# Two decoder layers on one core: 1/rms of the pre-norms moved behind the projections

## The chip, the core and the metric

The kernel runs on one core of one Trainium2 chip. The metric is the time of one execution in device microseconds (us); the median of several runs counts. The core's engines work in parallel, each through its own list of instructions in order: TensorE (PE: matmuls and transposes into PSUM; PEld is its loading of weights), VectorE (DVE), ScalarE (ACT), GpSimd (POOL) and SyncE (SP), which here only issues the DMA transfers. An instruction waits on semaphores for what it reads and for the buffer that it writes.

## The reference, cut to what matters

Two layers; x is 256 positions by 1024 columns, all in float32. Five norms stand in a layer. The three pre-norms (ahead of the mixer, the FFN and the gate) are the subject of the change; the two post-norms are touched on the side.

```python
def rms_norm(x, g, eps=1e-6):
    return x * rsqrt(mean(x * x, axis=-1) + eps) * g

for i in range(2):
    h = rms_norm(x, pre_mix_norm[i])                       # pre-norm 1
    z = h @ w_in[i]                                        # 1024 -> 2560 columns
    z_a, z_b, z_c, z_d = split(z, [768, 1280, 1792])
    out_a = rms_norm(moba_attention(rope(qa), rope(ka), va), out_norm_a[i])
    out_b = rms_norm(spatial_gating(gelu(z_b), ...), out_norm_b[i])
    out_c = rms_norm(conformer_conv(z_c, ...), out_norm_c[i])    # GLU, depthwise conv of 31 taps, ...
    out_d = diff_attention(rope(qd), rope(kd), vd)               # two softmax maps, per-head norm
    y = concat(out_a, out_b, out_c, out_d) @ w_out[i]
    x = x + rms_norm(y, post_mix_norm[i])                  # post-norm 1
    u = causal_dwconv(rms_norm(x, pre_ffn_norm[i]) @ w_up[i], ...)   # pre-norm 2; 5632 columns, 3 taps
    g, val = split(u, 2)
    f = (gelu(g) * val) @ w_down[i]
    x = x + rms_norm(f, post_ffn_norm[i])                  # post-norm 2
    gate = sigmoid(rms_norm(x, pe_gate_norm[i]) @ w_pe_gate[i])      # pre-norm 3
    x = x + gate * (p[i] @ w_pe_proj[i])
```

## The kernel before, in words

**Precision and weights.** A float32 matmul is made of three in the rounded type fp32r: each operand is split into hi (its rounding) and lo (the rest), and `mm3` (L322) adds hi·hi, hi·lo and lo·hi in PSUM. All weights are streamed once, in 208 pieces of 128x1024 (512 KB). For a piece `prep` (L297) issues the load (raw), ScalarE writes hi, and lo = raw - hi is formed by VectorE or, for the 71 pieces listed in POOL (L32), by GpSimd.

**Stages.** The positions lie as two row tiles t = 0, 1 of 128; x stays in SBUF (xs). A layer runs through `mixer` (L459; its steps in the order of the string STEPS, L36), `ffn` (L848) and `gate` (L907). The mixer's projections are made by `tok` (rows = positions: va and vd, bu and bv) or by `feat` (rows = features: the conv input ca and cg; dq, dk, aq, ak, which go through `rope`, L644). In the trace the y matmuls are the output projection, pj the small projection p[i] @ w_pe_proj, u the FFN's first projection (`up(j)`: 48 matmuls of 128x256 into one PSUM tile of 512 columns, for each of 22 j), f the second, gt the gate.

**A norm before.** For a row tile, ScalarE sums squares of two halves (`sumsq`, L413); GpSimd makes 1/rms (`rstd_of`, L403: mean plus eps, then a power of -0.5; in the trace a `_v` and a `_r`); VectorE multiplies xs by 1/rms and by the weight row g in two instructions of 128x512 (`norm_half`, L423: the tiles n_h, nf_h, ng_h for the three pre-norms); TensorE transposes the result in eight blocks of 128x128 into two PSUM tiles (n_t, nf_t, ng_t); ScalarE then writes hi and VectorE lo from PSUM, one 128x512 instruction each for every PSUM tile (`split_out`, L419: h_hi and h_lo, hf_, g_). The matmuls of the next stage read these, a block of 128 rows at a time. The weight rows g are loaded for each norm, 512 KB each (`load_gain`, L341).

**A post-norm before.** `post_norm_half` (L443) sums the squares of the two PSUM tiles of a row tile, multiplies them by g into SBUF tiles (pm_u for the mixer, pf_u for the FFN), and adds the product with 1/rms (pm_r, pf_r) to xs.

**The FFN's chain per j.** When the 48 u matmuls are done, ScalarE writes two uc of 128x256 from the PSUM tile (first tap and bias), VectorE adds four taps from PSUM (uc, 255 or 254 columns); then the PSUM tile is free. Gelu (ScalarE), product (VectorE), hi (ScalarE) and lo (VectorE) of f follow.

**Buffers.** PSUM has four tiles for y, f and gt, two for u and the mixer's projections (tag z) and two for transposes and small products (tag c). u j and u j+2 share a tile.

**Order.** The operations are recorded as the code runs (class Prog, L128), then issued in an order written out by hand, the string ORDER at the end of the file: a list of tokens such as `v.xs`, for the engine (s: ScalarE and the DMA issues of SyncE, v: VectorE, g: GpSimd, t: TensorE) and the tile. Every instruction therefore carries line L230, where `issue` ends up, and is told apart by its tiles. What each engine does in which order is decided by this string alone.

## Time and profile before

| | |
|---|---|
| median of 3 runs | 692.46 us (692.08 to 692.58) |
| profiled execution | 694.2 us |
| its span, first to last instruction | 692.5 us |
| mean granted TensorE clock | 0.992 |
| matmuls (transposes among them) | 4324 |
| HBM read | 118.23 MB, 172 GB/s over the span with the 1.05 MB written |
| weight pieces: load, hi, lo on VectorE, lo on GpSimd | 208, 208, 137, 71 |

In the profile's rows a group of instructions is given as engine, operation, output tile, "<-", input tiles and shape. In a list of groups the number, the busy us in all and the mean ns of one follow, then the idle time of the engine just before them with what ended it. In a stretch of the timeline a row begins with the start in us and the length, and ends with the count; a bracket holds how long the engine had waited and for whom. A table by stages has the window, its length, then for each engine the busy us and the number of instructions, the granted clock, the DMA share and GB/s. Layer 0 has its mixer from 0 to about 137 us, its FFN to about 320 and its gate to about 345; layer 1 follows in the same order.

### The profile page before, as it was taken

The numbers are of one execution on the slowest core, as the hardware profiler recorded it, in microseconds if no ns is written. First come the engines' busy times: TensorE is split into PE (matmuls) and PEld (weight loads), VectorE is DVE, ScalarE is ACT, GpSimd is POOL, SyncE is SP. The second block draws the span as 40 slices with busy tenths as digits, with TensorE's granted clock in tenths as the row PEclk, the third lists the DMA queues.
The fourth block names the chain that finished last, engine by engine and source line by source line (L and its number), as shares of the span: only waits on it lengthen the run. The fifth ranks groups of instructions, "written<-read, shape, count | busy, mean of one in ns | idle before, by whom it ended". The sixth has DMA issues, their size and how long they took to land.

```text
span 692.5 us, 11469 instructions
## 1 busy us (share of the span) xinstructions
PE 655.5 (95%) x4324; PEld 590.1 (85%) x4324; DVE 504.3 (73%) x873; ACT 414.6 (60%) x753; POOL 240.0 (35%) x181
## 2 busy tenths in 40 slices
...
GB/s 326 367 218 147 152 124 92 209 160 140 188 223 173 200 190 186 229 94 189 217 210 186 204 160 122 92 182 123 116 219 206 181 191 149 222 208 168 79 28 62
DMA packets 33750, 120.02 MB, mean 173 GB/s; under 512 B 3872, under 2 KB 4256, under 8 KB 33696
## 3 DMA queue, kind: packets, MB, share of 16 engines
...
HBM read 118.23 MB, written 1.05 MB: 172 GB/s over the span
## 4 chain that ended last, share of the span: by engine, by line
PE 42%; DVE 10%; ACT 2%; issue 1%; POOL 1%; POOLq 0%; DVEq 0%
PE u L230 16%; PE f L230 10%; PE gt L230 7%; DVE lo L230 2%; PE y L230 2%; DVE cacc L230 2%; DVE uc L230 1%; PE ca L230 1%; PE v L230 1%; PE cg L230 1%; PE aq L230 1%; PE ak L230 1%; DVE f L230 1%; DVE sw L230 1%; DVE nf_h L230 1%
## 5 line engine op out<-in xcount | busy, mean ns | idle before, releaser
L230 POOL TENSOR_TENSOR lo<-raw,hi 128x1024 fp32r<-128x1024 f32 x71 | 176.8, 2497 | 286.3 <-ACT hi L230 155.9
L230 ACT ACTIVATE hi<-raw 128x1024 fp32r<-128x1024 f32 x208 | 213.3, 1051 | 33.4 <-DMA raw<-in_wpk_dram 15.9
L230 DVE TENSOR_TENSOR lo<-raw,hi 128x1024 fp32r<-128x1024 f32 x137 | 178.3, 1322 | 29.0 <-ACT hi L230 22.2
L230 PE MATMUL u<-hf_hi,lo 128*128 128x256 f32 x704 | 197.1, 281 | 1.1 <-DVE lo L230 1.1
L230 PE MATMUL u<-hf_lo,hi 128*128 128x256 f32 x704 | 197.6, 281 | 0.0
L230 PE MATMUL u<-hf_hi,hi 128*128 128x256 f32 x704 | 196.4, 281 | 1.2 <-DVE uc L230 1.2
L230 PEld LDWEIGHTS u<-hf_hi,lo 128*128 128x128 f32 x704 | 132.4, 188 | 3.6 <-DVE lo L230 1.3
L230 PEld LDWEIGHTS u<-hf_hi,hi 128*128 128x128 f32 x704 | 132.1, 188 | 3.4 <-issue 1.4
L230 PEld LDWEIGHTS u<-hf_lo,hi 128*128 128x128 f32 x704 | 132.6, 188 | 2.6
L230 PE MATMUL f<-hi,f 128*128 128x512 f32 x352 | 120.2, 397 | 2.6 <-DVE f L230 2.6
L230 DVE SCALAR_TENSOR_TENSOR uc<-u,cols,uc 128x254 f32<-128x254 f32 (+1 forms) x176 | 79.0, 478 | 55.1 <-ACT uc L230 53.2
L230 ACT ACTIVATE uc<-u,cols 128x256 f32<-128x256 f32 x88 | 46.7, 559 | 57.1 <-PE u L230 53.5
L230 PEld LDWEIGHTS f<-hi,f 128*128 128x128 f32 x352 | 65.2, 189 | 14.0 <-DVE f L230 3.5
L230 PE MATMUL f<-lo,f 128*128 128x512 f32 x176 | 68.5, 396 | 0.0
L230 DVE SCALAR_TENSOR_TENSOR cacc<-cg,cols,cacc 128x253 f32<-128x253 f32 (+27 forms) x120 | 49.5, 458 | 3.2 <-ACT cacc L230 2.8
L230 ACT ACTIVATE uc<-uc 128x256 f32<-128x256 f32 x44 | 18.3, 415 | 39.4 <-DVE uc L230 39.2
L230 PEld LDWEIGHTS f<-lo,f 128*128 128x128 f32 x176 | 33.2, 189 | 5.6
L230 DVE TENSOR_TENSOR f<-uc,f 128x256 fp32r<-128x256 f32 x44 | 24.9, 569 | 11.4 <-ACT f L230 11.2
L230 DVE TENSOR_TENSOR uc<-uc 128x256 f32<-128x256 f32 x44 | 24.0, 546 | 11.5 <-ACT uc L230 10.3
L230 ACT ACTIVATE f<-uc 128x256 fp32r<-128x256 f32 x44 | 18.2, 413 | 22.6 <-DVE uc L230 22.5
L230 PE MATMUL gt<-hi,g_hi 128*128 128x512 f32 (+1 forms) x72 | 27.1, 379 | 0.0
L230 PE MATMUL gt<-lo,g_hi 128*128 128x512 f32 (+1 forms) x72 | 26.7, 372 | 0.0
...
## 6 DMA issues: line engine op xcount, KB each, us to landing
raw<-in_wpk_dram SPq DMA_DIRECT2D x208, 512.0 KB, 4.5
...
```

The lines of the kernel that those rows point to most:

```text
L230: getattr(getattr(tc.nc, o.eng), o.fn)(*[real(a) for a in o.args], **{k: real(v) for k, v in o.kw.items()})
```

## The change

1. **1/rms behind the projection.** The transposes take xs itself (`lift_half` replaces `norm_half`), so no n_h, nf_h or ng_h is made. 1/rms of a position is applied to the projection's result instead. Where positions are rows of the result, it is the scale of an instruction that was there: gelu, the values va and vd, and the gate's tanh (there with the factor 1/2 folded into the sum of squares). Where positions are columns, a row of 256 factors, equal in all partitions, is needed: `row_of` multiplies the unit matrix by 1/rms (mr_d before the mixer, qr_d before the FFN), one 128x128 for each row tile, multiplies these with a matrix of ones on TensorE in float32, and copies the sums to SBUF (mr, qr). With it VectorE multiplies, in PSUM, the conv input's two tiles (ca, cg) and each of the FFN's 22 u per layer (128x512, ahead of uc); the rotary tables are multiplied once per layer (tab_d, tab_a).
2. **Norm weights at the split.** After the transposes a feature is a partition, so g is a column: the hi's and lo's are made with this column (gc) as scale, in blocks of 128x128, eight of each per row tile instead of two. All columns come in one load of 128x48; three row loads of 512 KB per layer go.
3. **In PSUM.** The post-norm's product with g is written back over the PSUM tile, as are the rotary step's shuffle and its product with the sine table (before: SBUF tile sw).
4. **Order.** ORDER is written anew throughout, POOL has 74 pieces instead of 71, the tables of the rotary step are made at the start of the mixer (the step rt is gone from STEPS), and the SBUF tags hold 25 and 26 buffers (wt, w2) instead of 26 and 24.

```diff
+    ones = const([P, P], "ones", F32)
+    nc.gpsimd.memset(ones, 1.0)
...
-    def norm_half(t, g, hT, parts, nm):
+    def lift_half(t, n, hT, nm):
         hhi, hlo = hT
-        r = rstd_of(parts, 1e-6, nm)
-        hs = []
-        for c in range(2):
-            h = tmp(nm + "_h")
-            nc.vector.scalar_tensor_tensor(h, xs[:, t, c * 512:(c + 1) * 512], r, g[:, c * 512:(c + 1) * 512],
-                                           op0=ALU.mult, op1=ALU.mult)
-            hs.append(h)
         for c in range(2):
             ps = ctile(nm + "_t")
             for k in range(4):
-                nc.tensor.transpose(ps[:, k * P:(k + 1) * P], hs[c][:, k * P:(k + 1) * P], ident)
-            split_out(hhi[:, 4 * c:4 * c + 4, t * P:(t + 1) * P], hlo[:, 4 * c:4 * c + 4, t * P:(t + 1) * P],
-                      ps.rearrange("p (k n) -> p k n", n=P))
+                nc.tensor.transpose(ps[:, k * P:(k + 1) * P], xs[:, t, c * 512 + k * P:c * 512 + (k + 1) * P], ident)
+            for k in range(4):
+                g = gc[:, n * KT + 4 * c + k:n * KT + 4 * c + k + 1]
+                src, hi = ps[:, k * P:(k + 1) * P], hhi[:, 4 * c + k, tl]
+                nc.scalar.activation(hi, src, AF.Copy, scale=g)
+                nc.vector.scalar_tensor_tensor(hlo[:, 4 * c + k, tl], src, g, hi.bitcast(F32), op0=ALU.mult,
+                                               op1=ALU.subtract)
+
+    def row_of(rs, nm):
+        ps = ctile(nm)
+        for t in range(2):
+            dg = tmp(nm + "_d")[:, :P]
+            nc.vector.tensor_scalar(dg, ident, rs[t], None, op0=ALU.mult)
+            nc.tensor.matmul(ps[:, t * P:(t + 1) * P], ones, dg, start=True, stop=True)
+        row = tmp(nm)[:, :S]
+        nc.scalar.activation(row, ps[:, :S], AF.Copy)
+        return row, ps[:, :S]
...
     post_norm_half:
-            u = tmp(nm + "_u")
-            nc.vector.tensor_tensor(u, ys[c], g[:, c * 512:(c + 1) * 512], op=ALU.mult)
-            us.append(u)
+            nc.vector.tensor_tensor(ys[c], ys[c], g[:, c * 512:(c + 1) * 512], op=ALU.mult)
+            us.append(ys[c])
...
     mixer:
+        row, row_ps = row_of(rs, f"mr{i}")
+        for kind in ("d", "a"):
+            t_ = tmp(f"tab_{kind}{i}")
+            for m in range(2):
+                nc.vector.tensor_tensor(t_[:, m * S:(m + 1) * S], TC[kind][m], row_ps, op=ALU.mult)
+        def times_row(ps):
+            p3 = ps.rearrange("p (b s) -> p b s", s=S)
+            nc.vector.tensor_tensor(p3, p3, row[:, None, :].to_broadcast([P, 2, S]), op=ALU.mult)
...
     conf_in:
+            times_row(psg)
+            times_row(psa)
...
     rope:
-            sw = tmp("sw")
-            nc.vector.stream_shuffle(sw, ps, SWAP)
             nc.vector.tensor_tensor(a, ps3, ct[:, None, :].to_broadcast([P, 2, S]), op=ALU.mult)
-            sw3 = sw.rearrange("p (b s) -> p b s", s=S)
-            nc.vector.tensor_tensor(sw3, sw3, st[:, None, :].to_broadcast([P, 2, S]), op=ALU.mult)
-            nc.vector.tensor_tensor(a, a, sw3, op=ALU.add)
+            nc.vector.stream_shuffle(ps, ps, SWAP)
+            nc.vector.tensor_tensor(ps3, ps3, st[:, None, :].to_broadcast([P, 2, S]), op=ALU.mult)
+            nc.vector.tensor_tensor(a, a, ps3, op=ALU.add)
...
     ffn, up(j):
+            p3 = ps.rearrange("p (b s) -> p b s", s=S)
+            nc.vector.tensor_tensor(p3, p3, row[:, None, :].to_broadcast([P, 2, S]), op=ALU.mult)
...
     gate:
-                nc.scalar.activation(th, ps[:, ms], AF.Tanh, scale=0.5)
+                nc.scalar.activation(th, ps[:, ms], AF.Tanh, scale=rh[t])
```

Where the order is concerned, three places are shown. The first is VectorE at the end of the first mixer, from the post-norm to the split of the normed rows; y are the PSUM tiles of the output projection, pm_r is 1/rms of the post-norm and nf_r that of the pre-norm, raw, hi and lo the three forms of a weight piece. Before:

```order
L230 TENSOR_TENSOR pm_u<-y_1073,g_post_mix_1432 128x512
L230 TENSOR_TENSOR pm_u<-y_1167,g_post_mix_1432 128x512
L230 SCALAR_TENSOR_TENSOR xs<-pm_u,pm_r,xs 128x512 x2
L230 TENSOR_TENSOR lo_1472<-raw_1259,hi_1454 128x1024
L230 TENSOR_TENSOR pm_u<-y_1050,g_post_mix_1432 128x512
L230 SCALAR_TENSOR_TENSOR nf_h<-xs,nf_r,g_pre_ffn_1130 128x512 x2
L230 TENSOR_TENSOR pm_u<-y_1058,g_post_mix_1432 128x512
L230 SCALAR_TENSOR_TENSOR xs<-pm_u,pm_r,xs 128x512 x2
L230 TENSOR_TENSOR hf_lo<-nf_t,hf_hi 128x4x128
L230 SCALAR_TENSOR_TENSOR nf_h<-xs,nf_r,g_pre_ffn_1130 128x512 x2
L230 TENSOR_TENSOR hf_lo<-nf_t,hf_hi 128x4x128 x3
```

And now:

```order
L230 TENSOR_TENSOR y_1089<-y_1089,g_post_mix_1471 128x512
L230 SCALAR_TENSOR_TENSOR xs<-y_1089,pm_r,xs 128x512
L230 TENSOR_TENSOR y_1081<-y_1081,g_post_mix_1471 128x512
L230 SCALAR_TENSOR_TENSOR xs<-y_1081,pm_r,xs 128x512
L230 SCALAR_TENSOR_TENSOR hf_lo<-nf_t,gc,hf_hi 128x128
L230 TENSOR_TENSOR y_1161<-y_1161,g_post_mix_1471 128x512
L230 SCALAR_TENSOR_TENSOR hf_lo<-nf_t,gc,hf_hi 128x128 x3
L230 TENSOR_TENSOR y_1086<-y_1086,g_post_mix_1471 128x512
L230 SCALAR_TENSOR_TENSOR hf_lo<-nf_t,gc,hf_hi 128x128
L230 SCALAR_TENSOR_TENSOR xs<-y_1161,pm_r,xs 128x512
L230 SCALAR_TENSOR_TENSOR xs<-y_1086,pm_r,xs 128x512
L230 SCALAR_TENSOR_TENSOR hf_lo<-nf_t,gc,hf_hi 128x128 x11
```

The four nf_h are gone, the split is 16 steps of 128 columns (five of them ahead of the second row tile's xs), and the weight's lo has left this stretch.

The second is GpSimd at the same place; `_v` and `_r` are the two steps of a 1/rms. Before:

```order
L230 TENSOR_SCALAR pm_v<-pm_s 128x1
L230 TENSOR_TENSOR pm_r<-pm_v,nhalf 128x1
L230 TENSOR_SCALAR nf_v<-pm00x_s 128x1
L230 TENSOR_TENSOR nf_r<-nf_v,nhalf 128x1
L230 TENSOR_SCALAR pm_v<-pm_s 128x1
L230 TENSOR_TENSOR pm_r<-pm_v,nhalf 128x1
L230 TENSOR_SCALAR nf_v<-pm01x_s 128x1
L230 TENSOR_TENSOR nf_r<-nf_v,nhalf 128x1
L230 TENSOR_TENSOR lo_1581<-raw_1448,hi_1557 128x1024
```

And now:

```order
L230 TENSOR_SCALAR pm_v<-pm_s 128x1
L230 TENSOR_TENSOR pm_r<-pm_v,nhalf 128x1
L230 TENSOR_TENSOR lo_1539<-raw_1091,hi_1445 128x1024
L230 TENSOR_SCALAR pm_v<-pm_s 128x1
L230 TENSOR_TENSOR pm_r<-pm_v,nhalf 128x1
L230 TENSOR_TENSOR lo_1632<-raw_1095,hi_1144 128x1024
L230 TENSOR_SCALAR nf_v<-pm00x_s 128x1
L230 TENSOR_TENSOR nf_r<-nf_v,nhalf 128x1
L230 TENSOR_SCALAR nf_v<-pm01x_s 128x1
L230 TENSOR_TENSOR nf_r<-nf_v,nhalf 128x1
L230 TENSOR_TENSOR lo_1672<-raw_1093,hi_1479 128x1024
```

The pre-norm's two 1/rms now stand behind those of the post-norm and behind two lo's of weight pieces.

The third is VectorE at the first u of the FFN; qr_d are the two diagonals for the row of factors. Before:

```order
L230 TENSOR_TENSOR lo_1626<-raw_1596,hi_1624 128x1024
L230 TENSOR_TENSOR lo_1664<-raw_1266,hi_1450 128x1024
L230 TENSOR_TENSOR lo_1666<-raw_1508,hi_1657 128x1024
L230 SCALAR_TENSOR_TENSOR uc_1669<-u_1587,cols_187,uc_1669 128x255
L230 SCALAR_TENSOR_TENSOR uc_1669<-u_1587,cols_187,uc_1669 128x254
```

And now:

```order
L230 TENSOR_SCALAR qr_d<-ident,nf_r 128x128 x2
L230 TENSOR_TENSOR lo_1678<-raw_1588,hi_1674 128x1024
L230 TENSOR_TENSOR lo_1688<-raw_1593,hi_1683 128x1024
L230 TENSOR_TENSOR lo_1690<-raw_1520,hi_1686 128x1024
L230 TENSOR_TENSOR u_1620<-u_1620,qr_1697 128x512
L230 SCALAR_TENSOR_TENSOR uc_1717<-u_1620,cols_134,uc_1717 128x255
L230 SCALAR_TENSOR_TENSOR uc_1717<-u_1620,cols_134,uc_1717 128x254
```

Two diagonals are new ahead of the lo's, and the product of u with the row of factors stands between them and the first tap.

More of the change, by code (lines that the diff above doesn't have):

```diff
@@ L337, in tile_hymba @@
         load(xs[:, 0, c * 512:(c + 1) * 512], x[0:P, c * 512:(c + 1) * 512])
-    G_NAMES = ("pre_mix", "post_mix", "pre_ffn", "post_ffn", "gate")
+    G_NAMES = ("post_mix", "post_ffn")
     def load_gain(i, nm):
@@ L344, in load_gain @@
         return g
[L346 removed]
+    gc = const([P, 3 * L * KT], "gc", F32)
+    load(gc, gcol)
     while done[0] < RAW0:
@@ L441, in new_hT, with post_norm_half @@
                 nc.tile([P, KT, S], F32R, "big", nm + "_lo"))
-    def post_norm_half(t, ys, g, nm):
+    def post_norm_half(t, ys, g, nm, times=1.0):
         parts = [sumsq(ys[c], D, f"{nm}{c}") for c in range(2)]
@@ L454, in post_norm_half, with mixer @@
             nc.vector.scalar_tensor_tensor(xs[:, t, sl], us[c], r, xs[:, t, sl], op0=ALU.mult, op1=ALU.add)
-            nxt.append(sumsq(xs[:, t, sl], D, f"{nm}x{c}"))
+            nxt.append(sumsq(xs[:, t, sl], D, f"{nm}x{c}", times))
         return nxt
-    def mixer(i, hT):
+    def mixer(i, hT, rs):
         lam_init = 0.8 - 0.6 * math.exp(-0.3 * i)
@@ L845, in proj, with ffn @@
         return res
-    def ffn(i, hT, cl):
+    def ffn(i, hT, cl, rs):
         hhi, hlo = hT
+        row, _ = row_of(rs, f"qr{i}")
         g_post = load_gain(i, "post_ffn")
@@ L896, in ffn @@
                 down(j - 1, (0, 1))
-        g_gate = load_gain(i, "gate")
+        rg = []
         hG = new_hT(f"g{i}")
@@ L933, in gate @@
                 if c == 1:
-                    norm_half(t, g_next, hN, pp[t], f"n{i + 1}{t}")
-        return hN if i + 1 < L else None
-    hT = new_hT("h0")
+                    lift_half(t, 3 * (i + 1), hN, f"n{i + 1}{t}")
+                    rn.append(rstd_of(pp[t], 1e-6, f"n{i + 1}{t}"))
+        return (hN, rn) if i + 1 < L else None
+    hT, rs = new_hT("h0"), []
     for t in range(2):
+        lift_half(t, 0, hT, f"n0{t}")
         parts = [sumsq(xs[:, t, c * 512:(c + 1) * 512], D, f"x{t}{c}") for c in range(2)]
-        norm_half(t, g0, hT, parts, f"n0{t}")
+        rs.append(rstd_of(parts, 1e-6, f"n0{t}"))
+    nxt = hT, rs
     for i in range(L):
-        hF, cl, pj = mixer(i, hT)
-        hG = ffn(i, hF, cl)
-        hT = gate(i, hG, pj)
+        hF, cl, pj, rf = mixer(i, *nxt)
+        hG, rg = ffn(i, hF, cl, rf)
+        nxt = gate(i, hG, pj, rg)
     nc.issue(ctx, ORDER)
@@ new lines @@
+t.n00_t@4 s.h0_hi@12*3 s.raw2 s.raw0 s.raw1 v.h0_lo@13 v.h0_lo@12 s.cols0 s.h0_hi@15 v.h0_lo@15 s.x00_s s.x01_s
+t.n00_t@5*3 v.h0_lo@14 t.n00_t*2 s.h0_hi@5 v.h0_lo@5 s.h0_hi@6 v.h0_lo@6 s.h0_hi@4 v.h0_lo@4 t.n00_t*2 s.h0_hi v.h0_lo
+s.h0_hi s.h0_hi@3 v.h0_lo v.h0_lo@3 s.h0_hi*2 v.h0_lo@7 g.mask*2 g.ones g.nhalf g.posf g.n01_v g.ang g.ang@2 g.n01_r
+g.kf g.n00_v t.busy g.n00_r g.kf@2 v.h0_lo s.hi4 s.hi6 s.hi7 s.raw3 s.raw8 s.raw10 t.busy*18 s.hi5 s.first v.mr0_d
+g.kf*2 v.mr0_d v.lo4 t.mr0*2 v.lo6 v.ang s.mr0 v.lo7 t.busy v.ang v.ang@4 v.ang v.ang@5 v.ang*2 v.lo5 s.hi2 t.ca0
```

473 lines of the change are left out of this document (230 added, 243 removed).

## The prediction

> **What bounds the kernel now.** I read the page's engine lines first, then busy time by stage, then the waits of TensorE, then single stretches of the timeline.
>
> The page's first line has each engine's busy time, its share of the span and its instructions.
>
> ```profile
> PE 655.5 (95%) x4324; PEld 590.1 (85%) x4324; DVE 504.3 (73%) x873; ACT 414.6 (60%) x753; POOL 240.0 (35%) x181
> ```
>
> TensorE is busy for 655.5 of 692.5 us, so removing work elsewhere can give back at most the 37.0 us in which it stands still, unless it removes TensorE work; this change removes none. The stages show where those 37 us lie: start, length, then busy time of PE, PEld, DVE, ACT and POOL, then the granted clock.
>
> ```profile
> 0.00:17.00 17.00, 10.18 (x47) 9.15 (x48) 6.77 (x9) 7.96 (x16) 9.33 (x20) 1.00 0.87 325
> 52.00:104.00 52.00, 45.52 (x289) 37.82 (x288) 47.75 (x133) 34.58 (x89) 25.04 (x20) 0.97 0.40 140
> 104.00:138.00 34.00, 31.00 (x162) 25.09 (x161) 24.13 (x37) 24.22 (x62) 10.56 (x17) 1.00 0.45 152
> 138.00:294.00 156.00, 156.00 (x1144) 147.94 (x1144) 107.27 (x160) 93.97 (x138) 39.03 (x16) 1.00 0.57 187
> 294.00:364.00 70.00, 66.52 (x352) 56.11 (x351) 53.03 (x71) 40.69 (x73) 20.29 (x20) 0.98 0.54 176
> 381.00:450.00 69.00, 66.05 (x437) 56.53 (x436) 61.62 (x163) 48.55 (x126) 32.31 (x31) 1.00 0.44 144
> 450.00:503.00 53.00, 46.92 (x304) 41.62 (x303) 41.18 (x50) 34.07 (x57) 20.50 (x14) 1.00 0.44 145
> 503.00:623.00 120.00, 120.00 (x864) 112.97 (x863) 75.59 (x116) 67.69 (x101) 37.09 (x16) 1.00 0.58 195
> 623.00:674.00 51.00, 47.51 (x284) 41.78 (x283) 35.94 (x49) 26.33 (x48) 14.62 (x13) 0.97 0.29 94
> ```
>
> The two FFN stretches (138 to 294, 503 to 623) lose nothing: TensorE is their limit. The losses are the start (6.8), the first mixer (6.5 of 52 us, with VectorE at 47.75 of 52), and the places where a norm stands between two matmul stages: 3.0 before the first FFN, 3.5 around the first gate, 6.1 before the second FFN, 3.5 before the last gate; the second mixer loses 3.0. TensorE's waits name the same places (us in total, times, longest).
>
> ```profile
> PE n_t L230 <- DVE n_h L230: 7.5, 2, 5.4
> PE nf_t L230 <- DVE hf_lo L230: 4.3, 2, 2.6
> PE f L230 <- DVE f L230: 2.6, 2, 1.4
> PE nf_t L230 <- DVE nf_h L230: 2.3, 3, 1.0
> PE ng_t L230 <- DVE ng_h L230: 2.3, 1, 2.3
> ```
>
> The four norm rows are 16.4 us, 44% of the idle time. In each the transposes of the normed rows wait for VectorE. One such place, from post-norm to the first FFN matmul:
>
> ```profile
> 126.22 0.39 PE L230 MATMUL y<-hi,cat_lo 128*128 128x512 f32 x1
> 129.47 1.42 DVE L230 SCALAR_TENSOR_TENSOR xs<-pm_u,pm_r,xs 128x512 f32<-128x512 f32 x2 [0.24 <-POOL pm_r L230]
> 132.72 3.53 DVE L230 SCALAR_TENSOR_TENSOR nf_h<-xs,nf_r,g_pre_ffn 128x512 f32<-128x512 f32 x2 [1.23 <-POOL nf_r L230]
> 133.15 2.55 POOL L230 TENSOR_TENSOR lo<-raw,hi 128x1024 fp32r<-128x1024 f32 x1 [0.47 <-ACT hi L230]
> 136.90 0.66 PE L230 MATMUL nf_t<-ident,nf_h 128*128 128x128 f32 x4 [1.73 <-DVE hf_lo L230]
> 137.32 0.37 PE L230 MATMUL u<-hf_hi,hi 128*128 128x256 f32 x1
> ```
>
> From the last y matmul to the first u matmul pass 11.1 us; TensorE fills most with pj and transposes, not all. x is complete at 130.9, yet the transposes of its last quarter start at 136.9: sums of squares, 1/rms and nf_h lie between. And the two nf_h take 3.53 instead of the 1.42 of the equally large xs pair above, since GpSimd's lo began during them: both inputs of nf_h are in SBUF.
>
> **The change, part by part.** Prices come from these groups (count, busy us, mean ns):
>
> ```profile
> L230 DVE TENSOR_TENSOR lo<-raw,hi 128x1024 fp32r<-128x1024 f32 x137 | 178.3, 1322 | 29.0 <-ACT hi L230 22.2
> L230 DVE SCALAR_TENSOR_TENSOR n_h<-xs,n_r,g_pre_mix 128x512 f32<-128x512 f32 x8 | 7.9, 1029 | 12.0 <-POOL n_r L230 12.0
> L230 DVE TENSOR_TENSOR sw<-sw,sin_a 128x512 f32<-128x512 f32 x4 | 5.8, 1447 | 0.0
> L230 DVE TENSOR_TENSOR h_lo<-n_t,h_hi 128x512 fp32r<-128x512 f32 x8 | 5.5, 685 | 2.5 <-ACT h_hi L230 2.5
> L230 DVE TENSOR_TENSOR sw<-sw,sin_d 128x512 f32<-128x512 f32 x4 | 5.0, 1256 | 0.0
> L230 DVE TENSOR_TENSOR pm_u<-y,g_post_mix 128x512 f32<-128x512 f32 x8 | 5.4, 684 | 3.6 <-ACT pm_j L230 2.3 <-PE y L230 1.3
> L230 DVE SCALAR_TENSOR_TENSOR cat_lo<-ctt,cols,cat_hi 128x256 fp32r<-128x256 f32 x4 | 1.9, 482 | 7.3 <-ACT cat_hi L230 7.3
> L230 ACT ACTIVATE cat_hi<-ctt,cols 128x256 fp32r<-128x256 f32 x4 | 1.9, 474 | 0.8 <-DVE cat_lo L230 0.7
> L230 PE MATMUL cp<-cols,cs 128*128 128x256 f32 x16 | 4.1, 388 | 1.7 <-DVE cs L230 1.7
> ```
>
> *Norm boundaries.* The transposes now take x itself, so they may start at 130.9 in the stretch above instead of 136.9: 6 us off the chain. What comes back is the split in quarters: 16 pairs of 128x128 in place of four of 128x512 per norm. No row has a scaled split of 128 columns. Between nothing and cat_lo's 482 ns at 256, I extend the line from 685 at 512 through 482 at 256 to 380 at 128; on ScalarE likewise about 400. Eight per half of the rows are 3.0 us on VectorE against 1.4, and 3.2 on ScalarE; but the matmuls eat one 128-row block at a time, so only the first pair (0.8) is wholly exposed. The transposes' own order also shifts: half of them stand behind the y and pj matmuls that still run. So I leave each place a small rest: before the first FFN 3.0 becomes 0.6 (-2.4); the first gate and the next mixer 3.5 becomes 1.6, of which 1.4 is the f wait that the change does not touch (-1.9); before the second FFN 6.1 becomes 2.0 (-4.1); before the last gate 3.5 becomes 1.0 (-2.5). Together -10.9; at worst nothing, at best -14.7 with only the f wait left. GpSimd now has lo's between the 1/rms steps, 2.5 us each; pm_v waits behind one of them, and with it xs and the transposes, but y and pj matmuls that do not need x stand ahead of those.
>
> [...]
>
> *Start and first mixer.* The rows of the start:
>
> ```profile
> 7.00 0.63 ACT L230 ACTIVATE x_j<-xs 128x512 f32<-128x512 f32 x1 [4.92 <-DMA xs<-in_x_dram]
> 9.40 0.19 ACT L230 ACTIVATION_READ_ACCUMULATOR x_j<-xs 128x1 f32 x1
> 10.25 1.97 PE L230 MATMUL n_t<-ident,n_h 128*128 128x128 f32 x8 [5.38 <-DVE n_h L230]
> 16.69 0.36 PE L230 MATMUL ca<-h_lo,hi 128*128 128x256 f32 x1
> ```
>
> The wait of 5.4 for n_h goes, but ScalarE then makes the same four sums of squares (7.00 to 9.6) and 16 small hi's of 0.4 before the first weight is split: 16.0, where steady matmuls began at 16.69. I count nothing for the start itself. What counts is VectorE, nearly full from 52 to 104. Up to the step that scales the differential output (od) the order has five lo fewer on VectorE (-6.6), four n_h fewer (-4.1), four rotary products no longer SBUF with SBUF (5.4 to 2.7: -2.7); more are two row products on the conv input (+1.4), four table products of 256 columns (at the uc step's 0.48 below: +1.9), small lo's (16 x 0.38 - 4 x 0.685 = +3.3), and two diagonals (+0.6): -6.2. GpSimd has seven lo more in this mixer, 7 x 2.55 = 18 us, which slow the two-SBUF steps that stay; I give 2.2 back: -4.0, between 0 and -8.
>
> *Second mixer.* The same without the moved lo's: rotary -2.7 against +3.3 of row and table products, where TensorE itself is at 66 of 69 us: -1.0, between +1 and -3.
>
> *FFN.* Per pair j one product of 128x512 on PSUM is added, 44 x 0.684 = 30.1 us of VectorE. The 22 of a layer are 15.0 us, on top of 107.27 busy in 156 us; room enough on average, so I book no throughput. But it stands first in the chain that frees the PSUM bank of u:
>
> ```profile
> 143.64 0.57 ACT L230 ACTIVATE uc<-u,cols 128x256 f32<-128x256 f32 x1 [1.17 <-PE u L230]
> 145.64 1.91 DVE L230 SCALAR_TENSOR_TENSOR uc<-u,cols,uc 128x255 f32<-128x255 f32 x4 [0.70 <-ACT uc L230]
> 148.88 0.28 PE L230 MATMUL u<-hf_hi,hi 128*128 128x256 f32 x1
> ```
>
> u 0 is done when ScalarE begins at 143.64, its last tap ends at 147.55, 3.9 us later, and u 2 takes the bank again at 148.88: 1.3 us to spare in a run without down matmuls between. The product adds 0.7. The new order has more such runs: in each layer up to seven u's with at most a pair of down matmuls between two of them. I book +1.0 (0 to +8).
>
> *The rest.* Four 1/rms rows add eight float32 matmuls of 128 columns, under half of cp's 388 ns each: +1.6. Three gain loads per layer go, 512 KB each; DMA is not waited for. Post-norm products in PSUM cost what pm_u cost.
>
> Sum: -10.9 - 4.0 - 1.0 + 1.0 + 1.6 = -13.3. The profiled execution took 694.2 us, its span 692.5; the median of the runs is 692.46. I subtract from the median: 679.2, called **679.0**.
>
> **Rivals.** *The bank of u comes back late* (slower). VectorE and ScalarE work in order, and a lo of 1.3 us, or one slowed by GpSimd to over 2, may stand between product and taps. u 0 and u 1 fill 137.32 to 148.88, 5.8 us each. While the chain stays under that it costs nothing; at 6.6 each of about 30 u's in runs waits 0.8: +24, so 703. Against it: 3.9 now, 4.6 with the product, and a fifth of VectorE free. Chance 0.10.
>
> *The quarters cost what the norms gave*: hi and lo in small pieces hold ScalarE and VectorE, and half of the 10.9 stays: 684.5. For it: before the first FFN (104 to 138) VectorE and ScalarE are both busy for 24 of 34 us. Against it: 6 us leave the chain and the quarters add less than 2 to it. Chance 0.18.
>
> *The clock stays up*: three stretches with these gaps (86 to 104, 346 to 363, 658 to 675) have a low granted clock.
>
> ```profile
> 86.00:104.00 18.00, 14.72 (x78) 11.29 (x77) 13.99 (x39) 11.39 (x28) 6.87 (x7) 0.91 0.34 132
> 346.00:363.00 17.00, 14.92 (x72) 12.34 (x71) 11.98 (x15) 9.19 (x16) 3.20 (x3) 0.90 0.66 214
> 658.00:675.00 17.00, 14.74 (x66) 11.96 (x65) 12.16 (x14) 6.72 (x13) 3.54 (x5) 0.90 0.08 27
> ```
>
> A tenth of 52 us is 5.2; if gaps and low clock go together, 674. [...] Chance 0.15.
>
> *No change*: the first mixer's VectorE and the tail of each boundary absorb everything: 692.5. Chance 0.04.
>
> **How the numbers follow.** Forecast 0.53, by itself 674 to 684. The range 668 to 689 takes in the clock rival with mixers at their best (674 less a few us) and the quarters' rival with the bank chain at a few us; it leaves out the slow rival and no change. 0.2% is about what a measurement can tell, 1.4 us. Faster: 0.53 + 0.18 + 0.15 = 0.86; same 0.04; slower 0.10.
>
> **What would show it.** Right: the waits of n_t, nf_t and ng_t for VectorE fall below 5 us together; first u matmul within 7.5 us of the last y; FFN stretches still without idle; PE idle near 22 (37.0 less the first four terms). Wrong: waits of u for uc or for the row product over 5 us in total; TensorE idle in the FFN; mixers longer than before; VectorE time per norm growing past what nf_h gave back.

## The result and the profile after

The changed kernel takes 674.83 us (median of 4 runs, 674.68 to 675.71) against 692.27 for the kernel before beside it; the ratio is 0.9761 (95% interval 0.9731 to 0.9790). The profiled execution took 674.68 us, its span is 672.9, its mean granted clock 0.996. The forecast was 679.0, between 668 and 689: the sign and the range held. Its terms held only in part: the first gate came out with the other sign, the clock gave what no term had booked, and the experiments show that one part of the change, the split in quarters, costs up to 15 us, nearly as much as the whole change gains.

The page's engine line of the kernel after:

```profile
PE 653.2 (97%) x4340; PEld 589.6 (88%) x4340; DVE 493.2 (73%) x982; ACT 427.5 (64%) x827; POOL 236.7 (35%) x185
```

TensorE is idle for 19.7 of 672.9 us (37.0 before) and busy for 2.3 us less, although it has 16 instructions more in the records: the granted clock rose from 0.992 to 0.996 (see Clock, near the end).

TensorE's waits, as shown before: the n_h, nf_h and ng_h have left the list, and what stands for the norms is h_lo, g_lo, hf_lo and xs.

```profile
PE n_t L230 <- DVE h_lo L230: 3.1, 2, 2.1
PE gt L230 <- DVE g_lo L230: 2.2, 1, 2.2
PE u L230 <- DVE hf_lo L230: 1.3, 2, 1.0
PE n_t L230 <- DVE xs L230: 1.2, 1, 1.2
PE gt L230 <- ACT hi L230: 1.1, 1, 1.1
PE u L230 <- DVE uc L230: 0.5, 2, 0.3
```

The same stages of both kernels, each cut at its own matmuls: the ca from which on they run without a gap (in the kernel before the second one), the last y, the first u, the last f, the last n_t of the second layer, and so on. First after (start, length, then PE, PEld, DVE, ACT and POOL, clock, DMA share, GB/s):

```profile
0.00:16.82 16.82, 10.77 (x49) 9.21 (x49) 5.89 (x19) 10.19 (x27) 7.90 (x21) 1.00 0.85 308
16.82:118.86 102.04, 100.22 (x660) 87.84 (x659) 84.24 (x216) 79.32 (x175) 63.64 (x50) 1.00 0.52 183
118.86:124.82 5.96, 5.96 (x32) 4.92 (x31) 4.58 (x13) 5.89 (x19) 4.55 (x7) 1.00 0.92 296
124.82:314.76 189.94, 188.54 (x1333) 176.10 (x1332) 137.56 (x225) 113.11 (x180) 45.10 (x20) 1.00 0.54 179
314.76:348.90 34.14, 29.66 (x129) 22.96 (x127) 23.56 (x41) 20.50 (x46) 6.07 (x9) 0.95 0.64 216
348.90:447.80 98.90, 98.80 (x654) 87.68 (x655) 79.99 (x214) 69.03 (x166) 54.42 (x46) 1.00 0.42 142
447.80:454.92 7.12, 6.71 (x33) 4.84 (x32) 4.80 (x12) 6.13 (x18) 5.47 (x5) 1.00 0.82 296
454.92:644.40 189.48, 188.93 (x1333) 176.25 (x1334) 138.46 (x219) 112.51 (x178) 42.24 (x23) 1.00 0.52 173
644.40:672.90 28.50, 23.60 (x129) 19.82 (x127) 14.08 (x29) 10.79 (x27) 7.29 (x8) 0.96 0.10 37
```

And the six stages of before that differ most, cut alike:

```profile
16.69:126.45 109.76, 103.28 (x651) 89.37 (x649) 93.52 (x215) 78.21 (x169) 52.36 (x44) 0.98 0.51 183
126.45:137.32 10.87, 7.87 (x42) 5.81 (x40) 9.15 (x11) 7.24 (x16) 5.04 (x7) 1.00 0.74 243
326.50:360.12 33.62, 31.54 (x143) 25.50 (x142) 26.56 (x32) 19.87 (x34) 6.00 (x9) 0.96 0.73 234
360.12:457.40 97.28, 94.33 (x628) 82.80 (x628) 79.89 (x194) 62.67 (x150) 46.54 (x40) 1.00 0.46 149
457.40:468.44 11.04, 7.31 (x38) 5.41 (x36) 9.97 (x12) 7.45 (x17) 5.07 (x6) 1.00 0.51 177
468.44:664.66 196.22, 190.38 (x1335) 177.35 (x1336) 134.16 (x190) 111.46 (x170) 61.42 (x27) 0.99 0.50 167
```

The differences of the lengths add up to the span: first mixer -7.7, its norm -4.9, first FFN +0.8 (189.18 before), first gate +0.5, second mixer +1.6, second norm -3.9, second FFN with the last gate's norm -6.7, start +0.1, end +0.7; together -19.6. A length also changes when matmuls move across a cut (eight nf_t now stand inside the second mixer, ahead of its norm) and with the clock. TensorE's idle time, length less PE, does not have the first fault. By it the first gate lost 2.4 us (2.08 before, 4.48 after) and the second mixer gained 2.9 (2.95 before, 0.10 after).

The first gate is where the change should have gained and did not. There the transposed tile is split like this (start, length, engine; in the bracket the wait):

```profile
323.14 0.37 ACT L230 ACTIVATE g_hi<-ng_t,gc 128x128 fp32r<-128x128 f32 x1 [2.50 <-DVE g_lo L230]
323.54 0.35 DVE L230 SCALAR_TENSOR_TENSOR g_lo<-ng_t,gc,g_hi 128x128 fp32r<-128x128 f32 x1 [0.43 <-ACT g_hi L230]
323.92 0.37 ACT L230 ACTIVATE g_hi<-ng_t,gc 128x128 fp32r<-128x128 f32 x1 [0.42 <-DVE g_lo L230]
325.29 0.73 PE L230 MATMUL gt<-hi,g_hi 128*128 128x512 f32 x2 [1.15 <-ACT hi L230]
328.41 0.50 PE L230 MATMUL gt<-hi,g_lo 128*128 128x512 f32 x1 [2.16 <-DVE g_lo L230]
```

The table of the stretch right behind:

```profile
329.40:332.60 3.20, 3.20 (x9) 2.42 (x8) 1.80 (x5) 1.36 (x3) 1.72 (x3) 0.50 0.49 160
```

A hi waits for the lo before it, although it neither reads nor overwrites what that lo writes: both read the same PSUM tile. So the two engines take turns, 0.78 us for a block, where a run of eight takes either engine 0.27 for each (the rows of his_first below). The first wait is longer, 2.50 us, since the lo that it is for stood behind two lo's of weights on VectorE (from 318.79, 4.05 us): taking turns also makes one engine wait for what stands in the other's queue. TensorE loses 3.3 us, and then, as the row of the table shows, runs at half its clock (0.50 granted). In the trace each of these waits (0.42 and 0.43 us, and the 2.50) is released by the other engine's step on the same tile; what lies behind the release was not shown.

### The profile page after: what moved, and what is told of

Read it like the earlier page. It is cut to its first block, busy times and chain, and to the rows that moved or that the text cites. A ratio compares the mean times of both kernels' runs of the same rounds, so it can differ in the third digit from the quotient of the medians.

```text
span 672.9 us, 11683 instructions
## 1 busy us (share of the span) xinstructions
PE 653.2 (97%) x4340; PEld 589.6 (88%) x4340; DVE 493.2 (73%) x982; ACT 427.5 (64%) x827; POOL 236.7 (35%) x185
## 4 chain that ended last, share of the span: by engine, by line
PE 81%; DVE 8%; ACT 8%; issue 1%; DMA 1%; POOL 0%; DVEq 0%; ACTq 0%
PE u L230 33%; PE f L230 16%; PE y L230 6%; PE gt L230 5%; PE v L230 3%; PE b L230 3%; DVE lo L230 2%; PE ak L230 2%; PE dq L230 2%; PE aq L230 2%; PE ca L230 2%; PE dk L230 2%; PE cg L230 2%; DVE uc L230 1%; ACT hi L230 1%
## 5 line engine op out<-in xcount | busy, mean ns | idle before, releaser
L230 POOL TENSOR_TENSOR lo<-raw,hi 128x1024 fp32r<-128x1024 f32 x74 | 181.2, 2464 | 286.8 <-ACT hi L230 144.4
L230 DVE TENSOR_TENSOR lo<-raw,hi 128x1024 fp32r<-128x1024 f32 x134 | 171.3, 1294 | 24.3 <-ACT hi L230 13.6
L230 PE MATMUL f<-hi,f 128*128 128x512 f32 x352 | 113.0, 395 | 0.0
L230 DVE SCALAR_TENSOR_TENSOR uc<-u,cols,uc 128x255 f32<-128x255 f32 (+1 forms) x176 | 80.7, 479 | 39.4 <-ACT uc L230 37.4
L230 DVE SCALAR_TENSOR_TENSOR cacc<-cg,cols,cacc 128x255 f32<-128x255 f32 (+28 forms) x120 | 50.7, 462 | 2.3 <-ACT cacc L230 1.1
L230 DVE TENSOR_TENSOR u<-u,qr 128x512 f32<-128x512 f32 x44 | 30.6, 696 | 24.6 <-PE u L230 23.6
L230 PE MATMUL gt<-hi,g_lo 128*128 128x512 f32 (+1 forms) x72 | 27.0, 382 | 2.2 <-DVE g_lo L230 2.2
```

The source lines that it names most:

```text
L230: getattr(getattr(tc.nc, o.eng), o.fn)(*[real(a) for a in o.args], **{k: real(v) for k, v in o.kw.items()})
```

## The experiments

Theory A, from the prediction: the gain comes from taking 1/rms and the scaled copy out of the way from x to the transposes, and from VectorE's relief in the mixers; quarters, product on u and rows cost little. Theory B: the rewritten order and GpSimd's list give the gain, not the arithmetic. Each run stands beside the kernel before on the same chip; that one's median was 690.5 to 692.3, so differences of under 2 us between runs on different chips are not told apart.

Stage lengths in the profiled executions, in us, cut at the first ca, the last y, the first u, the last f, the first v of layer 1, and so on:

| | before | after | his_first | halves | row_twice | sbuf_products | lo_back | psum_products | norm_first | new_in_old_order |
|---|---|---|---|---|---|---|---|---|---|---|
| start | 15.3 | 16.8 | 14.1 | 13.1 | 16.8 | 16.8 | 17.4 | 15.3 | 28.1 | 14.9 |
| first mixer | 110.9 | 101.8 | 101.2 | 101.3 | 101.8 | 113.1 | 120.5 | 108.9 | 107.1 | 114.7 |
| its norm | 11.1 | 6.2 | 6.8 | 6.2 | 6.2 | 8.1 | 8.5 | 11.5 | 14.6 | 9.4 |
| first FFN | 188.9 | 189.7 | 189.6 | 188.2 | 195.8 | 189.7 | 189.7 | 190.8 | 186.4 | 204.4 |
| gate to v | 63.1 | 66.8 | 62.0 | 59.7 | 66.8 | 68.3 | 66.8 | 61.9 | 85.4 | 68.6 |
| rest of mixer | 67.8 | 66.3 | 66.3 | 66.3 | 66.3 | 75.4 | 66.3 | 66.6 | 65.4 | 69.2 |
| its norm | 11.2 | 7.3 | 7.5 | 6.5 | 7.3 | 10.5 | 7.3 | 10.6 | 26.8 | 8.6 |
| second FFN | 196.0 | 189.2 | 189.1 | 188.5 | 200.8 | 194.8 | 189.3 | 194.6 | 190.1 | 212.8 |

### The split in quarters

**halves.** The four blocks of a PSUM tile are split at once; this leaves the norm weight out of the result.

```diff
-            for k in range(4):
-                g = gc[:, n * KT + 4 * c + k:n * KT + 4 * c + k + 1]
-                ...
+            split_out(hhi[:, 4 * c:4 * c + 4, tl], hlo[:, 4 * c:4 * c + 4, tl], ps.rearrange("p (k n) -> p k n", n=P))
```

> The changed kernel with the split in one step of 128x512 per PSUM tile on each engine instead of four of 128x128; the norm weight is left out of the result, since a column can't be applied to four blocks at once. If the quarters cost the norms part of their gain (16 hi and 16 lo per norm hold ScalarE and VectorE, and ScalarE and VectorE take turns on a tile), 668 to 672 us, most of it at the start (10.5 us from the first hi to the last lo now) and at the first gate (waits of 4.5 us now). If the early first quarter is worth as much as the smaller number of steps, 674 to 676.

659.67 us, ratio 0.9541 (0.9502 to 0.9580): 15.2 us faster than the changed kernel, and below both expected ranges. The start gives 3.7, the stretch from gate to v 7.1, and the clock is 1.000.

**his_first.** Only the order of the issue changes: in each PSUM tile the four hi come ahead of the first lo.

```diff
-s.h0_hi@9 s.h0_hi@8 v.h0_lo@9 ... v.h0_lo@8 s.h0_hi@11 v.h0_lo@11 s.h0_hi@10 v.h0_lo@10
+s.h0_hi@9 s.h0_hi@8 s.h0_hi@11 s.h0_hi@10 v.h0_lo@9 ... v.h0_lo@8 v.h0_lo@11 v.h0_lo@10
```

> The changed kernel in which the four hi of a PSUM tile are issued ahead of its first lo; nothing else is changed. In the trace of the changed kernel a hi waits for the lo that was issued ahead of it on the same PSUM tile, 0.42 us each time, so a block takes 0.78 us in turn where each engine alone needs 0.26. If these turns cost time on the path, the start's split shrinks from 10.5 us by 3 to 5 and the first gate's wait by 1 to 2: 669 to 673 us. If the first pair of a tile, which comes 0.5 us later now, or the weights' hi behind it on ScalarE set the end, 674 to 676.

666.54 us, ratio 0.9640 (0.9601 to 0.9680), 8.3 us faster than the changed kernel and below the expected 669 to 673: with nothing but the order of the issue it beats both kernels. The split of the start, in the changed kernel first (its first three rows and its last; the last lo ends at 15.99):

```profile
5.45 0.60 ACT L230 ACTIVATE h_hi<-n_t,gc 128x128 fp32r<-128x128 f32 x2
6.09 0.61 DVE L230 SCALAR_TENSOR_TENSOR h_lo<-n_t,gc,h_hi 128x128 fp32r<-128x128 f32 x2 [6.09 <-ACT h_hi L230]
6.73 0.37 ACT L230 ACTIVATE h_hi<-n_t,gc 128x128 fp32r<-128x128 f32 x1 [0.68 <-DVE h_lo L230]
15.38 0.61 DVE L230 SCALAR_TENSOR_TENSOR h_lo<-n_t,gc,h_hi 128x128 fp32r<-128x128 f32 x2 [0.69 <-ACT h_hi L230]
```

and with the hi first, all 16 blocks:

```profile
5.40 2.16 ACT L230 ACTIVATE h_hi<-n_t,gc 128x128 fp32r<-128x128 f32 x8
6.56 2.16 DVE L230 SCALAR_TENSOR_TENSOR h_lo<-n_t,gc,h_hi 128x128 fp32r<-128x128 f32 x8 [6.56 <-ACT h_hi L230]
8.89 2.18 ACT L230 ACTIVATE h_hi<-n_t,gc 128x128 fp32r<-128x128 f32 x8
10.06 0.87 DVE L230 SCALAR_TENSOR_TENSOR h_lo<-n_t,gc,h_hi 128x128 fp32r<-128x128 f32 x3 [1.35 <-ACT h_hi L230]
11.10 1.38 DVE L230 SCALAR_TENSOR_TENSOR h_lo<-n_t,gc,h_hi 128x128 fp32r<-128x128 f32 x5 [0.17 <-ACT h_hi L230]
```

10.5 us become 7.1: ScalarE works on one PSUM tile while VectorE works on the other. So these steps on different PSUM tiles don't wait for each other: from 6.56 to 7.56 both engines run. The turns are worth 8.3 of the 15.2; the other 6.9 are the smaller number of steps together with the weight that halves leaves out, which these runs don't separate.

**g_in_psum.** The weight is applied to the whole PSUM tile by one VectorE product, then the split is made by halves.

```diff
+            g = gc[:, n * KT + 4 * c:n * KT + 4 * c + 4]
+            nc.vector.tensor_tensor(ps3, ps3, g.unsqueeze(2).to_broadcast([P, 4, P]), op=ALU.mult)
+            split_out(hhi[:, 4 * c:4 * c + 4, tl], hlo[:, 4 * c:4 * c + 4, tl], ps3)
```

> The changed kernel with the norm weight applied in PSUM: one VectorE product of 128x512 with the weight's columns per PSUM tile (24 in all), then one hi and one lo of 128x512 instead of four each. If what the quarters cost is the number of steps and the turns of the two engines, and one step of 0.69 more per tile is all that comes back of it: the 659.7 us of the split by halves plus 0.7 at the start, at each of the five places and in the mixers together some 3 us: 661 to 665. If the chain product, hi, lo (2.0 us per tile against 0.8 for the first quarter) is too long for the stages' beginnings: 667 to 672.

668.98 us, ratio 0.9681 (0.9655 to 0.9706): within the second expectation. It beats the changed kernel by 5.9 and loses 2.4 to his_first.

**g_first.** x is multiplied by the weight row ahead of the transposes; halves after them.

```diff
+            nc.vector.tensor_tensor(h, xs[:, t, c * 512:(c + 1) * 512], g[:, c * 512:(c + 1) * 512], op=ALU.mult)
-                nc.tensor.transpose(ps[:, k * P:(k + 1) * P], xs[:, t, c * 512 + k * P:c * 512 + (k + 1) * P], ident)
+                nc.tensor.transpose(ps[:, k * P:(k + 1) * P], hs[c][:, k * P:(k + 1) * P], ident)
```

> The changed kernel with x multiplied by the norm weight ahead of the transposes (128x512 on VectorE, two per row tile, both inputs in SBUF, the weight rows loaded as in the kernel before) and the split by halves; 1/rms stays behind the projection. It puts the step n_h back on the way from x to the transposes, but not the sums and 1/rms. Where GpSimd runs a lo beside it, a pair took 3.53 us in the kernel before, and 1.42 where it didn't. If a step ahead of the transposes is what delays the stages: 1 to 2 us at each of the five places and at the start, 666 to 672. If only the sums and 1/rms mattered: 660 to 664.

699.88 us, ratio 1.0130 (1.0096 to 1.0164): far outside both ranges, 40 us above halves for 24 steps. Their groups:

```profile
L230 DVE TENSOR_TENSOR nf_h<-xs,g_pre_ffn 128x512 f32<-128x512 f32 x8 | 14.4, 1800 | 0.3
L230 DVE TENSOR_TENSOR ng_h<-xs,g_gate 128x512 f32<-128x512 f32 x8 | 11.7, 1465 | 0.3
L230 DVE TENSOR_TENSOR n_h<-xs,g_pre_mix 128x512 f32<-128x512 f32 x8 | 5.5, 714 | 8.3 <-DMA g_pre_mix<-in_gains_dram 8.2
```

The same product takes 714 ns at the pre-mixer norms and 1800 ns ahead of the FFN, where the order has GpSimd's lo's: in the trace a step takes 1.9 to 2.8 us beside such a lo and 0.69 without one. At the start the step waits 8.2 us for the weight row's load (third row), a load that the changed kernel doesn't have. One step on this way is dear, and dearer beside GpSimd; but the step also shifts everything behind it in the queues, so its own share is not separated.

### The product with 1/rms in the FFN

**no_row** leaves the product out, and with it the FFN's 1/rms; **row_twice** multiplies every u by the row twice.

```diff
 no_row:     -            nc.vector.tensor_tensor(p3, p3, row[:, None, :].to_broadcast([P, 2, S]), op=ALU.mult)
 row_twice:  +            nc.vector.tensor_tensor(p3, p3, row[:, None, :].to_broadcast([P, 2, S]), op=ALU.mult)
```

> The changed kernel without the 44 products of u with the row of 1/rms (128x512 on PSUM, 0.70 us each, 30.6 us in all), so that 1/rms of the FFN's norm is left out of the result. Theory A (the product is hidden behind TensorE, since the bank of u comes back in time): 674 to 675.5 us, no change. Rival (the product delays the banks and VectorE's other work in the FFN): 671 to 673.

673.23 us, ratio 0.9742 (0.9693 to 0.9791), between the two expectations: 1.6 us less than the changed kernel, little, and not clear of the intervals. Theory A's "hidden" holds to about that.

> The changed kernel with every u multiplied twice by the row of 1/rms (the factor is squared in the FFN): 44 more products, 30.6 us more of VectorE, and 0.7 us more in the chain that frees the bank of u. The first chains of the changed kernel end with 0.6 to 3 us to spare in runs of u without down matmuls. Theory A (spare time of about 1 to 2 us at most places): 675 to 680 us. If the chain was already at its limit as the slow rival had it, each of some 30 u in runs waits 0.7 more: 690 or more.

692.28 us, ratio 1.0019 (0.9999 to 1.0039): 17.5 us above the changed kernel, as the rival had it. The price group of the changed kernel, and TensorE's waits with the product made twice:

```profile
L230 DVE TENSOR_TENSOR u<-u,qr 128x512 f32<-128x512 f32 x44 | 30.6, 696 | 24.6 <-PE u L230 23.6 <-ACT qr L230 1.0
```

```profile
PE u L230 <- DVE lo L230: 6.2, 6, 3.2
PE u L230 <- DVE uc L230: 5.2, 7, 1.1
```

The first 30.6 us of VectorE cost at most 1.6, the second 17.5. The waits name both ways: the bank (uc) and the weights (a lo behind the products). So the forecast's slow rival was real in kind and lay one product away; the larger share of the waits, though, is for weights and not for the bank.

### The products in PSUM

**sbuf_products** undoes the third part in the changed kernel; **psum_products** makes it alone in the kernel before.

```diff
 sbuf_products, post-norm:
-            nc.vector.tensor_tensor(ys[c], ys[c], g[:, c * 512:(c + 1) * 512], op=ALU.mult)
+            u = tmp(nm + "_u")
+            nc.vector.tensor_tensor(u, ys[c], g[:, c * 512:(c + 1) * 512], op=ALU.mult)
 and the rotary shuffle into an SBUF tile sw; psum_products: the reverse
```

> Of the changed kernel only the third part is undone: the post-norm's product, the rotary shuffle and the product with the sine table go to SBUF tiles again, order and all else as changed. If these products in PSUM gave what was booked (2.7 us of VectorE in each mixer, since with both inputs in SBUF the two products of a mixer grow from 0.7 to 1.3 us each beside GpSimd), 677 to 679 us; if TensorE no longer waits for VectorE in the mixers anyway, 674.5 to 676.

705.52 us, ratio 1.0226 (1.0170 to 1.0281): 31 us above the changed kernel, some ten times what was expected. The steps that read these products, in the changed kernel (three groups) and here, and TensorE's longest wait here:

```profile
L230 DVE SCALAR_TENSOR_TENSOR xs<-y,pm_r,xs 128x512 f32<-128x512 f32 x8 | 5.7, 747 | 0.7 <-POOL pm_r L230 0.7
L230 DVE SCALAR_TENSOR_TENSOR xs<-f,pf_r,xs 128x512 f32<-128x512 f32 x8 | 5.9, 750 | 2.2 <-POOL pf_r L230 2.0
L230 DVE TENSOR_TENSOR rot_dk<-rot_dk,dk 128x512 f32<-128x512 f32 x2 | 1.4, 686 | 0.1
```

```profile
L230 DVE SCALAR_TENSOR_TENSOR xs<-pm_u,pm_r,xs 128x512 f32<-128x512 f32 x8 | 18.3, 2316 | 0.8 <-POOL pm_r L230 0.7
L230 DVE SCALAR_TENSOR_TENSOR xs<-pf_u,pf_r,xs 128x512 f32<-128x512 f32 x8 | 10.8, 1355 | 2.5 <-POOL pf_r L230 2.3
L230 DVE TENSOR_TENSOR rot_dk<-rot_dk,sw_dk 128x512 f32<-128x512 f32 x2 | 5.6, 2787 | 0.1
PE nf_t L230 <- DVE xs L230: 10.5, 6, 2.1
```

With u in SBUF the addition to x has both inputs in SBUF; the changed order has a lo on GpSimd right behind pm_r, and the step grows from 747 to 2316 ns. The mixers lose 11.3 and 9.1 us. Beside a lo that GpSimd had begun 0.07 us earlier, a single xs took 2.85 us here (at 124.4) and 0.75 in the changed kernel (at 115.1).

> The kernel before with the third part of the change alone: post-norm product, rotary shuffle and sine product stay in PSUM; the order is that of before, with the sine table made ahead of its first use. By the ledger, 2.7 us of VectorE less in each mixer, part of it on the path: 1 to 5 us faster than before. By the loss of 31 us that undoing it in the changed kernel gave, it would be far more, 10 to 30 us faster; but that loss was measured in an order whose lo's on GpSimd run beside these products, so in the old order little should come: 0 to 5 us faster.

690.04 us, ratio 0.9979 (0.9964 to 0.9994): 1.9 us faster than before, as expected. The same part is worth 2 us in one order and 31 in the other. By these two runs it buys little time by itself, but the freedom to put GpSimd's lo's beside these steps.

### Order or arithmetic

**norm_first** puts 1/rms back ahead of the transposes in the changed kernel and drops all rows and products; **new_in_old_order** issues the changed arithmetic in the order of before.

```diff
 norm_first:
+            nc.vector.tensor_scalar(h, xs[:, t, c * 512:(c + 1) * 512], r, None, op0=ALU.mult)
-                nc.tensor.transpose(ps[:, k * P:(k + 1) * P], xs[:, t, c * 512 + k * P:c * 512 + (k + 1) * P], ident)
+                nc.tensor.transpose(ps[:, k * P:(k + 1) * P], hs[c][:, k * P:(k + 1) * P], ident)
 new_in_old_order: POOL of before; ORDER of before, h_hi, h_lo and the like four times each, new tokens inserted
```

> Of the changed kernel only 1/rms is put back ahead of the transposes: per row tile two products of 128x512 on VectorE (n_h and its like, without the weight, which stays at the split), no rows of factors, no products on u, on the conv input or on the tables; the order is the changed kernel's, with 1/rms and its products as soon as their sums are there and the transposes behind them. Theory A (the gain came from taking 1/rms out of the way from x to the transposes): the waits of n_t, nf_t and ng_t for VectorE come back, 3 us at the start and about 2 at each of the five places between stages, less some 1 us for the rows that go: 684 to 690 us. Theory B (the gain came from the rewritten order, the POOL list and the smaller loads, not from the arithmetic): 674 to 679.

753.64 us, ratio 1.0926 (1.0888 to 1.0964). TensorE's waits:

```profile
PE nf_t L230 <- DVE nf_h L230: 20.7, 5, 5.2
PE n_t L230 <- DVE n_h L230: 16.7, 5, 4.4
PE ng_t L230 <- DVE ng_h L230: 13.7, 4, 5.7
```

The direction is Theory A's: the start, the norms and the gates are long again, the FFNs are not (the first, free of the products, is 2.5 below the kernel before). The size is not: 79 us above the changed kernel. TensorE's idle time is 58 us longer (77.8 for 19.7); the other 20 are busy time, at a mean clock of 0.957 for 0.996. One reason shows before the first FFN (rows of the timeline):

```profile
130.30 2.34 POOL L230 TENSOR_TENSOR lo<-raw,hi 128x1024 fp32r<-128x1024 f32 x1
130.37 2.95 DVE L230 TENSOR_SCALAR nf_h<-xs,nf_r 128x512 f32<-128x512 f32 x2 [1.84 <-POOL nf_r L230]
141.49 4.83 POOL L230 TENSOR_TENSOR lo<-raw,hi 128x1024 fp32r<-128x1024 f32 x2
141.56 5.05 DVE L230 TENSOR_SCALAR nf_h<-xs,nf_r 128x512 f32<-128x512 f32 x2 [1.86 <-POOL nf_r L230]
```

The changed order puts a GpSimd lo right behind nf_r. Both times it begins 0.07 us before nf_h and stretches the pair, 0.48 us each at the pre-mixer norms, to 2.95 us, and to 5.05 beside two lo's.

> The changed kernel's arithmetic in the order and with the POOL list of the kernel before; every token that both have stands where it stood, the quarters of a split stand where the half stood, new operations right ahead of the first one that needs them, and the sine table of the differential heads is made earlier. Theory A: TensorE's waits for normed rows are gone although nothing was reordered for it, and with the mixers' VectorE no better (its lo's stay): 679 to 685 us. Theory B: little is left of the gain, 688 us or more, since the new products and quarters stand in an order not made for them.

733.15 us, ratio 1.0634 (1.0592 to 1.0676). Here the norms are shorter than before (9.4 and 8.6 for 11.1 and 11.2), as Theory A has it, and the rest is mostly longer, the FFNs by 15.5 and 16.8. TensorE's longest wait there:

```profile
PE f L230 <- ACT f L230: 15.0, 9, 5.0
```

The down matmuls wait for f, whose chain now begins with a product that the order of before had no place for; that this product is the cause is argued, not tested. So neither theory holds by itself. The new arithmetic shortens the norms in either order, and of these runs it pays only with the order made for it; both mixtures are slower than the kernel before. norm_first is not quite the old arithmetic, since it keeps the quarters and the products in PSUM. How many of the 17.4 us belong to order and how many to arithmetic can't be read from these two runs, and the smaller loads and the buffer counts were not tried by themselves.

### The first mixer

**lo_back** gives nine of the first mixer's lo's back to VectorE.

```diff
-POOL = (1, 3, 8, 9, 10, ..., 17, 18, 20, 21, 22, 23, 25, 26, 32, ...)
+POOL = (10, ..., 18, 20, 21, 32, ...)
```

> Of the changed kernel only nine lo's of the first mixer's weights (pieces 1, 3, 8, 9, 17, 22, 23, 25, 26) go back from GpSimd to VectorE, at their place in the order. If the first mixer's gain came from the relief of VectorE, its 84 of 102 us there become 95 and TensorE waits again: 678 to 683 us. If it came from the shorter norm chain and the order alone, 675 to 677.

695.75 us, ratio 1.0080 (1.0049 to 1.0111). The loss, 21 us, is mostly one wait, and a low clock around it (a wait of TensorE, and the stretch from 17 to 52 us):

```profile
PE b L228 <- DVE lo L228: 10.9, 1, 10.9
17.00:52.00 35.00, 24.02 (x134) 21.23 (x134) 28.83 (x47) 16.57 (x23) 7.40 (x6) 0.80 0.55 194
```

A lo moved from GpSimd's queue into VectorE's stands behind 20 steps of the convolution there (8.9 us), and TensorE waits for it. That is mostly the fault of one place, not the price of nine lo's, so the run doesn't decide.

**psum_and_lo** tries the other way: psum_products with the same nine lo's on GpSimd, each right behind its hi.

```diff
+POOL of before and (1, 3, 8, 9, 17, 22, 23, 25, 26)
```

> The kernel before with the third part of the change (products in PSUM) and with nine lo's of the first mixer's weights (pieces 1, 3, 8, 9, 17, 22, 23, 25, 26) on GpSimd, right behind their hi; norms and order else as before. The part alone ran 2 us faster than before, its first mixer 108.9 us from the first ca matmul to the last y, against 110.9 before and 101.8 changed. If what shortens the first mixer is VectorE rid of these nine lo's (11.7 us) while its rotary products no longer collide with GpSimd, the stage falls to 102 to 105 and the time to 683 to 687 us. If it is the rewritten order of the mixer, or 1/rms and n_h out of the way, the stage stays at 107 to 110 and the time at 688 to 692.

700.28 us, ratio 1.0135 (1.0104 to 1.0167): slower, the first mixer 121.1 us. After the start no wait is longer than 2.6 us; there are many, and the clock is 0.93 to 0.95 from 17 to 138 us. So the nine lo's alone don't shorten the first mixer in the old order.

## Why the forecast came out right, step by step

The terms were booked as idle time of TensorE, so they are held against its idle time (length less PE, cut as in the tables above; the stages of before that are not shown there are cut alike):

| | booked | idle before | idle after | change |
|---|---|---|---|---|
| start | 0 | 6.8 | 6.1 | -0.8 |
| first mixer | -4.0 | 6.5 | 1.8 | -4.7 |
| its norm | -2.4 | 3.0 | 0.0 | -3.0 |
| first FFN | +1.0 for both | 1.4 | 1.4 | 0.0 |
| first gate | -1.9 | 2.1 | 4.5 | +2.4 |
| second mixer | -1.0 | 3.0 | 0.1 | -2.9 |
| its norm | -4.1 | 3.7 | 0.4 | -3.3 |
| second FFN with the last gate's norm | -2.5 | 5.8 | 0.5 | -5.3 |
| end | none | 4.7 | 4.9 | +0.2 |
| together | -14.9 | 37.0 | 19.7 | -17.3 |

The signs that the forecast had named for being right all came: the waits of n_t, nf_t and ng_t for VectorE are 4.5 us together, the first u stands 6.0 and 7.1 us behind the last y, and the FFNs have as little idle time as before or less. But part of the waiting only moved on from the transposes to the next matmuls (gt for g_lo 2.2, u for hf_lo 1.3), which the first sign doesn't count.

**Norm boundaries.** The mechanism was right: transposes take x as soon as it is there, and the last y to first u takes 6.0 us for 10.9. Three of the four places came close to their terms: -3.0, -3.3, and 2.3 before the last gate (the wait of ng_t for ng_h, now gone) for -2.5. The rest of the last FFN's -5.3 is some 3.5 us of waits of f for f, u for lo and u for uc that lie outside the forecast's stretch "503 to 623", so that it took the FFN to lose nothing; 0.3 of them are left. The fourth place, "the first gate and the next mixer 3.5 becomes 1.6", failed: 2.1 of these 3.5 lie in the gate, and they became 4.5.

**The quarters** are what failed there: "the quarters add less than 2" to the chain and "only the first pair (0.8) is wholly exposed". The price of a step was right (346 and 368 ns for the estimates 380 and 400). What the working lacked is that hi and lo of one PSUM tile wait for each other, so that four blocks cost 3.1 us in turns; cat_lo's row had shown it (ScalarE's cat_hi waiting 0.7 for cat_lo). With the hi's first the gate's idle time is 1.8. Measured over the whole kernel: 8.3 us for the turns, up to 15 in all. The rival that gave the quarters 5.5 was right in kind and too small.

**Luck.** That the time still came out 4 us below the forecast, and not above it, is luck in part: the quarters were booked too cheap, and the second mixer, the last FFN and the clock, which nothing in the sum had priced, gave more than was booked.

**Start and first mixer.** Booked -4.0; the mixer's idle time fell by 4.7 and its busy time by 3.1, of which about 1.7 is one stretch of low clock less (an estimate, see Clock). The ledger of VectorE's work gave the sign: VectorE is busy 84.2 us there for 93.5. Which part of the order gives the gain stays open: two attempts to move the lo's alone made the mixer 12 to 19 us longer.

**FFN.** Booked +1.0, "0 to +8"; leaving the product out gave 1.6. Right, with less to spare than the forecast's chance of 0.10 for the slow rival would suggest (row_twice).

**Rows.** "Eight float32 matmuls" for +1.6 are sixteen in the trace (mr and qr, eight each) and take 2.6 us.

**Products in PSUM.** "Post-norm products in PSUM cost what pm_u cost" was right of the product (694 and 692 ns for 684) and missed the step behind it: the addition to xs loses one of its two SBUF inputs. In the changed order that is worth 31 us with the rotary steps.

**Clock.** The rival's 5 us came by more than half: the kernel before has three stretches of 3.4 us at a granted clock of 0.50 (from 88.0, 357.7 and 661.4), the changed kernel one (from 329.4; a further one, from 670.7, lies behind its last matmul). Two less are worth about 3.4 us, an estimate from half of 3.4 us each. halves and his_first, with 9.7 and 14.5 us of idle time, have a mean clock of 1.000. The forecast's upper bound, 37.0 us of standing still, left this out: the span fell by 17.3 us of idle and 2.3 us of busy time.
